# Rounded products for the RG-LRU gates and the mLSTM numerators, a last chunk through DRAM, and mixer blocks transposed a step later

## The chip, the cores and the metric

The kernel runs on one core of one Trainium2 chip. A time is the device time of one execution in microseconds. TensorE (PE) does the matrix products, VectorE (DVE), ScalarE (ACT) and GpSimd (POOL) the elementwise work, and SyncE (SP) starts the loads of the weights; GpSimd also starts some transfers of its own queue. All of them run at the same time and wait for one another by semaphores; each works through its own list in order.

## The reference

A decoder trunk of two layers works on 256 tokens of width 2048, batch 1, everything in fp32. Each layer takes an RMS norm, one combined input projection, token mixers, a gate, an output projection added to the residual, and then a gated embedding from a second input. Layer 0 has two mixers side by side on 1024 channels each: HGRN2 (a linear recurrence with a state matrix, in chunks of 64) and the RG-LRU:

```python
r  = sigmoid(einsum('bsnc,ncd->bsnd', xh, w_r) + b_r)     # 8 blocks of 128 x 128
ig = sigmoid(einsum('bsnc,ncd->bsnd', xh, w_i) + b_i)
log_a = -LRU_C * r * softplus(-lam)
a = exp(log_a);  u = sqrt(-expm1(2.0 * log_a)) * (ig * xf)
h_t = a_t * h_(t-1) + u_t
```

Layer 1 has an mLSTM of 8 heads (keys of 128, values of 256 channels): scores of queries and keys with a causal weight from two gates, a numerator (weights times values) and a denominator (the sum of the weights). The gate path is a product with SiLU of another projection.

## The kernel before, in words

Every weight matrix is read from HBM once, in halves of 128 x 1024 (`raw`, five buffers, L128). fp32 products are made of three products of a rounded format (fp32r): ScalarE rounds a half into `whi` (L131), VectorE subtracts to get the rest, `wlo` (L132); both have four buffers. The activations stand as pairs of the same kind (`ahl`, made by `split_act`: L145 rounds on ScalarE, L146 subtracts on VectorE). TensorE then adds up hi·hi, hi·lo and lo·hi. There are two forms. `block` makes 128 output channels by 256 tokens: sixteen matmuls of 512 columns (L161, weights hi against both halves of the activations), and sixteen of 256 (L167, weights lo). `quarter_tok` makes a quarter of the sum for 512 channels by 256 tokens: 24 matmuls of 512 columns (L225 to L227), twelve for each half of the tokens, from two weight halves. `project_tok` is four quarters, and `project_two` two chunks with the fourth quarters last.

The small work between is written as generators, one list of them per lane. `pump()` steps every lane once; it stands in the middle of each `block` and each `quarter_tok`. So the order of work around the products is set by how many `yield`s a generator has, and a tile scheduler then orders each engine's list by priority (weight splits have a raised one).

Layer 0 runs 32 blocks: the forget gates, queries and the RG-LRU inputs, between them two token-major chunks, then two chunks of the gate `ez` (`gate_tok`) and the other gate blocks (`gate_mul`), and the output projection `eo`. `rg_lru(r, xc)` runs for two halves of 512 channels. It loads the gates' weights `bw` (128 x 1024), waits a step (two for r = 1), and makes the gates in plain fp32: four matmuls at L823 for each of two `j`, an fp32 matmul being two records in the trace. After these come sigmoids (L827), exponentials (L833, L834) and the scan (L846).

`feature_major` turns a gated chunk of tokens by channels into channels by tokens: VectorE transposes blocks of 32 (L520), `across` writes it to DRAM and reads it back (L507, L510, on POOL's queue), and after a lag of five steps ScalarE applies a gain (L527) and it is split. Layer 1's last chunk goes another way, `feature_major_pe`: eight transposes on TensorE (L542), read from PSUM by the splits.

In layer 1 `mix(j)` (j = 0 to 3, two heads each) makes the causal weights `wt`, the scores (L1058, L1059), their product `scw`, and in the next step the numerators in plain fp32 (L1070, L1072: 257 columns, 256 values and a column of ones for the denominator). Values `vt` are written from the projection `ov` by ScalarE, the ones by POOL (L1099). After `oz`, the embedding's product (L338) runs, then `drain("fm0", ... "fm3")` finishes the chunks and `out_proj` multiplies with `oo`. POOL loads two rows of gains (`row`, L367) for L1151, which multiplies the embedding's values on VectorE while `oo` runs.

Of the kernel before, what the change touches and what calls it, by code (L numbers as in the profile page):

```python
# [19 lines left out]
P = 128  # L20
# [23 lines left out]
def trunk(ctx: ExitStack, tc: tile.TileContext, a, out):  # L44
# [368 lines left out]
    def out_proj(hq, w, y, lane):  # L413

        act = {}
        for c in range(4):
            ps = project_tok(w, c, y)
            with tc.high_priority(offset=100):
                for hf in range(2):
                    v.tensor_tensor(out=hq[c][:, hf], in0=ps[hf], in1=hq[c][:, hf], op=ALU.add)  # L420
            start(f"{lane}{c}", to_features(hq[c], c, act, None, lane))
            step(f"{lane}{c}")
        return act
# [91 lines left out]
    def feature_major(u, gain, first, y, room):  # L515

        w = room("w")
        w5 = w.rearrange("p (j c h t) -> p h c j t", j=4, c=4, h=2)
        for hf in range(2):
            v.transpose(w5[:, hf], u[:, hf].rearrange("p (c j q) -> p c j q", c=4, j=4))  # L520
        r = room("r")
        yield from across(w, r, f"du{gain}{first}", 5)
        r5 = r.rearrange("p (i c h t) -> p c h i t", i=4, c=4, h=2)
        for b in range(2):
            x = tp.tile([P, 512], F32, name="xr", tag="hn", bufs=3)
            for k in range(2):
                s.activation(x[:, k * T:(k + 1) * T].rearrange("p (h i t) -> p h i t", h=2, i=4), r5[:, 2 * b + k],  # L527
                             AF.Copy, scale=pc(gain, first + 2 * b + k))
            y[first // 2 + b] = split_act(x, "y")

    def feature_major_pe(u, gain, first, y):

        yield
        yield
        banks = []
        for b in range(2):
            ps = px.tile([P, 512], F32, name="mx", tag="mx")
            for k in range(2):
                c = (2 * b + k) * P
                for hf in range(2):  # L540
                    o = k * T + hf * P
                    te.transpose(ps[:, o:o + P], u[:, hf, c:c + P], ident)  # L542
            banks.append(ps)
        yield
        for b, ps in enumerate(banks):
            hi, lo, both = act_pair()
            for k in range(2):
                scaled_split(ps[:, k * T:(k + 1) * T], gain, first + 2 * b + k, hi[:, k], lo[:, k])
            y[first // 2 + b] = (hi, lo, both)
# [55 lines left out]
    with m0_scope:  # L605
# [203 lines left out]
        def rg_lru(r, xc):  # L809
# [6 lines left out]
            if r:  # L816
                yield
            for j in range(2):
                for w, (dst, bias) in enumerate(((av, "bbr"), (it, "bbi"))):
                    ps = px.tile([P, 512], F32, name="mx", tag="mx")  # L820
                    for i in range(2):
                        c = 2 * j + i
                        te.matmul(ps[:, i * T:(i + 1) * T], bw[:, w, c * P:(c + 1) * P], xc[:, c * T:(c + 1) * T],  # L823
                                  start=True, stop=True)
# [92 lines left out]
    act = out_proj(hq, a["eo"], y, "fe")  # L917
# [30 lines left out]
    with tc.tile_pool(name="m1", bufs=2) as m1:  # L948
# [39 lines left out]
        VW = 257  # L988
# [49 lines left out]
        def mix(j):  # L1038
# [15 lines left out]
            scw = room("scw")[:, 0:768].rearrange("p (i t) -> p i t", i=2)  # L1054
            for i in range(2):
# [7 lines left out]
            vt = vts[j]  # L1063
            nm = m1.tile([P, 2, 512], F32, name="num", tag="vt", bufs=6)
            for i in range(2):
                pool, tag = ((px, "mx"), (pst, "st"))[i]
                for hf in range(2):
                    c = hf * 8 + 2 * j + i
                    ps = pool.tile([P, 512], F32, name="nu", tag=tag)[:, 0:VW]
                    te.matmul(ps, scw[:, i, hf * P:(hf + 1) * P], vt[:, 0, i], start=True, stop=(hf == 0))  # L1070
                    if hf:
                        te.matmul(ps, scw[:, i, T:384], vt[:, 1, i], start=False, stop=True)  # L1072
                    o = nm[:, hf, i * 256:(i + 1) * 256]
                    s.copy(o, ps[:, 0:256])
                    v.tensor_copy(den[:, c:c + 1], ps[:, 256:VW])
# [20 lines left out]
        for j in range(4):  # L1096
            psv = project_tok(a["ov"], j, acth)
            vt = m1.tile([P, 2, 2, VW], F32, name="vt", tag="vt", bufs=6)
            gp.memset(vt[:, :, :, 256:VW], 1.0)  # L1099
            for hf in range(2):  # L1100
                s.activation(vt[:, hf, :, 0:256], psv[hf].rearrange("p (i e) -> p i e", i=2), AF.Copy,
                             scale=norm["rt"][:, hf:hf + 1])
            vts.append(vt)
# [18 lines left out]
        for j in range(4):  # L1122
# [8 lines left out]
            start(f"fm{j}", feature_major(u, "cn", 4 * j, y, room) if j < 3 else feature_major_pe(u, "cn", 4 * j, y))  # L1131
# [229 lines left out]
```

## Time and profile before

| what | us |
|---|---|
| median of 3 runs (lowest, highest) | 1051.79 (1050.85, 1053.89) |
| the profiled execution | 1051.14 |
| its span in the trace | 1049.4 |
| TensorE busy | 1038.6 |
| VectorE busy | 724.3 |
| ScalarE busy | 594.3 |
| GpSimd busy | 114.4 |

The span is one execution as the profiler saw it; some 1.7 us lie around it. The granted TensorE clock was 0.998 over the span. A row of the timeline has the start, the duration, the engine, the line of the code and the operation, what is written and read, and how many alike were joined; in brackets stands the idle time ahead of it and what ended it. A matmul's duration is modelled and longer than the distance to its successor, since matmuls overlap.

### The profile page before, as it was taken

What the parts mean: (1) busy time and instruction counts of PE and PEld (TensorE: products, weight loads), DVE (VectorE), ACT (ScalarE), POOL (GpSimd) and SP (SyncE); (2) the same over time, 40 slices, a digit from 0 to 9 for tenths busy, and PEclk for the clock granted to TensorE, in tenths of its full rate; (3) what the DMA queues carried; (4) which work ended last, traced back from release to release, by engine and by line L of the source; (5) the groups of instructions that cost most, each with busy time, mean ns of one, the idle gap of its engine ahead of it and who ended that gap; (6) DMA issues with size and microseconds to landing.
All of it is one profiled execution on the core that took longest, in us unless ns stands there. A gap on an engine that the chain in (4) does not pass through costs nothing.

```text
span 1049.4 us, 14961 instructions
## 1 busy us (share of the span) xinstructions
PE 1038.6 (99%) x5504; PEld 869.1 (83%) x5504; DVE 724.3 (69%) x1085; ACT 594.3 (57%) x893; POOL 114.4 (11%) x162
## 2 busy tenths in 40 slices
PE   9999999999999999999999999999999999999996
PEld 7888888888888888887888788888888888888886
DVE  6857897997877666766569864454457767666675
ACT  7775545869654444565557765544445565444553
POOL 0001232522201111111021000000001110111000
PEclk9999999999999999999999999999999999999999
DMA  9865544545867877687597644446557775977652
GB/s 350 311 205 192 172 164 157 182 150 192 275 234 258 249 247 230 212 277 235 177 271 248 203 169 160 161 161 201 199 188 225 250 262 187 294 239 242 201 181 81
DMA packets 64587, 225.40 MB, mean 215 GB/s; under 512 B 8065, under 2 KB 9345, under 8 KB 64513
## 3 DMA queue, kind: packets, MB, share of 16 engines
q1 hardware_dynamic: 55440, 196.38, 56.5%
q0 software_dynamic: 8496, 27.27, 8.6%
q8 instruction: 43, 0.70, 0.3%
q10 hardware_dynamic: 576, 0.79, 0.2%
q14 instruction: 32, 0.25, 0.1%
HBM read 211.30 MB, written 13.11 MB: 214 GB/s over the span
## 4 chain that ended last, share of the span: by engine, by line
PE 97%; DMA 1%; ACT 1%; DVE 0%; issue 0%; SPq 0%; ACTq 0%
PE mm L225 22%; PE mm L226 22%; PE mm L227 22%; PE mm L161 11%; PE mm L167 6%; PE mx L225 2%; PE mx L227 2%; PE mx L226 2%; PE mm L338 1%; DMA xq<-in_xT_dram 1%; PE mm L1196 1%; PE mm L1195 1%; PE mm L1194 1%; PE mx L823 1%; PE nu L1070 1%; PE mx L661 0%
## 5 line engine op out<-in xcount | busy, mean ns | idle before, releaser
L132 DVE TENSOR_TENSOR wlo<-raw,whi 128x1024 fp32r<-128x1024 f32 (+1 forms) x364 | 439.9, 1220 | 246.4 <-ACT whi L131 211.3
L131 ACT CAST whi<-raw 128x1024 fp32r<-128x1024 f32 (+1 forms) x364 | 378.3, 1043 | 356.4 <-PE mm L227 254.8
L225 PE MATMUL mm<-whi,ahl 128*128 128x512 f32 x1024 | 401.5, 392 | 0.0
L227 PE MATMUL mm<-whi,ahl 128*128 128x512 f32 x1024 | 398.5, 389 | 0.0
L226 PE MATMUL mm<-wlo,ahl 128*128 128x512 f32 x1024 | 398.4, 389 | 0.0
L225 PEld LDWEIGHTS mm<-whi,ahl 128*128 128x128 f32 x1024 | 192.2, 188 | 42.0 <-issue 2.1
L227 PEld LDWEIGHTS mm<-whi,ahl 128*128 128x128 f32 x1024 | 192.2, 188 | 40.5
L226 PEld LDWEIGHTS mm<-wlo,ahl 128*128 128x128 f32 x1024 | 192.3, 188 | 39.8 <-DVE wlo L132 0.5
L161 PE MATMUL mm<-ahl,whi 128*128 128x512 f32 x512 | 122.1, 390 | 0.0
L161 PEld LDWEIGHTS mm<-ahl,whi 128*128 128x128 f32 x512 | 94.2, 188 | 18.3
L167 PE MATMUL mm<-ahl,wlo 128*128 128x256 f32 x512 | 67.7, 285 | 0.0
L167 PEld LDWEIGHTS mm<-ahl,wlo 128*128 128x128 f32 x512 | 64.9, 191 | 2.2
L225 PE MATMUL mx<-whi,ahl 128*128 128x512 f32 x96 | 37.5, 391 | 0.0
L227 PE MATMUL mx<-whi,ahl 128*128 128x512 f32 x96 | 37.4, 389 | 0.0
L226 PE MATMUL mx<-wlo,ahl 128*128 128x512 f32 x96 | 37.3, 389 | 0.0
L507 POOL DMA_DIRECT2D ducn<-w x3 | 1.7, 561 | 206.2 <-DVE w L520 206.2
L173 ACT COPY sm<-mm 128x256 f32<-128x256 f32 x32 | 11.7, 366 | 19.1 <-PE mm L167 19.0
L225 PEld LDWEIGHTS mx<-whi,ahl 128*128 128x128 f32 x96 | 18.0, 188 | 3.7
L227 PEld LDWEIGHTS mx<-whi,ahl 128*128 128x128 f32 x96 | 18.0, 188 | 3.8
L226 PEld LDWEIGHTS mx<-wlo,ahl 128*128 128x128 f32 x96 | 18.0, 188 | 3.7
L971 DVE SCALAR_TENSOR_TENSOR qk<-xr,prm,qk 128x255 f32<-128x255 f32 (+2 forms) x48 | 20.4, 475 | 0.6 <-ACT qk L968 0.5
L1195 PE MATMUL mm<-wlo,ahl 128*128 128x256 f32 x64 | 18.1, 283 | 0.0
(304 smaller groups left out, 877.3 us busy)
## 6 DMA issues: line engine op xcount, KB each, us to landing
raw<-in_ew_dram SPq DMA_DIRECT2D x64, 512.0 KB, 4.4
raw<-in_g_dram SPq DMA_DIRECT2D x56, 512.0 KB, 4.7
raw<-in_eo_dram SPq DMA_DIRECT2D x32, 512.0 KB, 4.8
raw<-in_oqk_dram SPq DMA_DIRECT2D x32, 512.0 KB, 4.6
raw<-in_ov_dram SPq DMA_DIRECT2D x32, 512.0 KB, 3.8
raw<-in_oog_dram SPq DMA_DIRECT2D x32, 512.0 KB, 3.7
raw<-in_oz_dram SPq DMA_DIRECT2D x32, 512.0 KB, 4.2
raw<-in_oo_dram SPq DMA_DIRECT2D x32, 512.0 KB, 4.5
```

Of the source, the lines that this page charges most:

```text
L131: last["act"] = s.copy(h, r).ins
L132: last["dve"] = v.tensor_tensor(out=l, in0=r, in1=h.bitcast(F32), op=ALU.subtract).ins
L161: last["pe"] = te.matmul(ps, parts[k // 8][0][:, c:c + P], act[k // 2][2][:, (k % 2) * 512:(k % 2 + 1) * 512], start=(k == 0), stop=False).ins
L167: last["pe"] = te.matmul(ps[:, T:2 * T], parts[k // 8][1][:, c:c + P], act[k // 2][0][:, k % 2], start=False, stop=(k == KT - 1)).ins
L173: s.copy(small, ps[:, T:2 * T])
L225: te.matmul(ps[hf], xh, wh, start=(k == 0), stop=False)
L226: te.matmul(ps[hf], xh, wl, start=False, stop=False)
L227: last["pe"] = te.matmul(ps[hf], xl, wh, start=False, stop=(k == KT - 1)).ins
L338: last["pe"] = te.matmul(ps[hf], tokens(pact[x], k, hf), (hi, lo)[y][:, k * 512:(k + 1) * 512], start=(n == mine[0]), stop=(n == mine[-1]) ...
L823: te.matmul(ps[:, i * T:(i + 1) * T], bw[:, w, c * P:(c + 1) * P], xc[:, c * T:(c + 1) * T], start=True, stop=True)
L971: v.scalar_tensor_tensor(dst[:, sh:T], pi[:, 0:T - sh], pc("ccw", k * 16 + n), dst[:, sh:T], op0=ALU.mult, op1=ALU.add)
L1195: te.matmul(ps[hf], xh, wl, start=False, stop=False)
```

## The change

There are four parts. They touch the layer-0 gates, the layer-1 numerators, the last layer-1 chunk, and the two layer-0 chunks that go through DRAM.

1. In `rg_lru`, `bw` is split into a rounded part and a rest that take one `whi` and one `wlo` buffer, and the input `xc` is split into two pairs. The four plain matmuls for each `j` become twelve rounded ones (`mm3`), and they come one step later.
2. In `mix`, the weights `wt` are multiplied in place by the scores and split into `sh` and `sl`; the values are rounded as `vt`, with the rest in `vl`. Six matmuls for two heads become 18. The values have 258 columns now, two of them ones; the rest `vl` has 256.
3. `feature_major_pe` is gone: the last chunk goes through DRAM like the others. The output projection `oo` runs through `chunks`, which takes the first two chunks of output together, and steps a chunk's lane only where its values are needed.
4. The layer-0 chunks are transposed a step later, and the lag behind their transfer is four instead of five.

```diff
-    def out_proj(hq, w, y, lane):
+    def out_proj(hq, parts, lane):
         act = {}
-        for c in range(4):
-            ps = project_tok(w, c, y)
+        for c, ps in enumerate(parts):
...
-    def feature_major(u, gain, first, y, room):
+    def feature_major(u, gain, first, y, room, lag):
+        if lag < 5:
+            yield
         w = room("w")
...
-        yield from across(w, r, f"du{gain}{first}", 5)
+        yield from across(w, r, f"du{gain}{first}", lag)
...
-    def feature_major_pe(u, gain, first, y):
-        yield
-        yield
-        banks = []
-        for b in range(2):
-            ps = px.tile([P, 512], F32, name="mx", tag="mx")
-            for k in range(2):
-                c = (2 * b + k) * P
-                for hf in range(2):
-                    o = k * T + hf * P
-                    te.transpose(ps[:, o:o + P], u[:, hf, c:c + P], ident)
-            banks.append(ps)
-        yield
...
     def rg_lru(r, xc):
...
             if r:
                 yield
+            bh, bl = (wp.tile([P, 2, 512], F32R, name=n, tag=n) for n in ("whi", "wlo"))
+            s.copy(bh, bw)
+            v.tensor_tensor(out=bl, in0=bw, in1=bh.bitcast(F32), op=ALU.subtract)
+            xs = [split_act(xc[:, j * 512:(j + 1) * 512], "xc") for j in range(2)]
+            yield
...
-                        te.matmul(ps[:, i * T:(i + 1) * T], bw[:, w, c * P:(c + 1) * P], xc[:, c * T:(c + 1) * T],
-                                  start=True, stop=True)
+                        mm3(ps[:, i * T:(i + 1) * T], bh[:, w, c * P:(c + 1) * P], bl[:, w, c * P:(c + 1) * P], xs[j], i,
+                            True, True)
...
-                start(f"fm{g}", feature_major(u, "an", 4 * g, y, room0))
+                start(f"fm{g}", feature_major(u, "an", 4 * g, y, room0, 4))
...
-        VW = 257
+        VW = 258
...
-            scw = room("scw")[:, 0:768].rearrange("p (i t) -> p i t", i=2)
...
-                v.scalar_tensor_tensor(scw[:, i, :], sc[:, 0:384], SC, wt[:, i, :], op0=ALU.mult, op1=ALU.mult)
+                v.scalar_tensor_tensor(wt[:, i, :], sc[:, 0:384], SC, wt[:, i, :], op0=ALU.mult, op1=ALU.mult)
+            sh, sl = (bp.tile([P, 1024], F32R, name=n, tag="wt")[:, 0:768].rearrange("p (i t) -> p i t", i=2)
+                      for n in ("sh", "sl"))
+            s.copy(sh, wt)
+            v.tensor_tensor(out=sl, in0=wt, in1=sh.bitcast(F32), op=ALU.subtract)
             yield
...
-                    te.matmul(ps, scw[:, i, hf * P:(hf + 1) * P], vt[:, 0, i], start=True, stop=(hf == 0))
-                    if hf:
-                        te.matmul(ps, scw[:, i, T:384], vt[:, 1, i], start=False, stop=True)
+                    for b, o in ((0, hf * P), (1, T))[:1 + hf]:
+                        for x, y, n in ((sh, vh, VW), (sl, vh, VW), (sh, vl, T)):
+                            te.matmul(ps[:, 0:n], x[:, i, o:o + P], y[:, b, i], start=(b == 0 and x is sh and y is vh),
+                                      stop=(b == hf and y is vl))
...
-            vt = m1.tile([P, 2, 2, VW], F32, name="vt", tag="vt", bufs=6)
+            vt = m1.tile([P, 2, 2, VW], F32R, name="vt", tag="vt", bufs=6)
...
+                v.scalar_tensor_tensor(vl[:, hf], src, norm["rt"][:, hf:hf + 1], vt[:, hf, :, 0:256].bitcast(F32),
+                                       op0=ALU.mult, op1=ALU.subtract)
...
-            start(f"fm{j}", feature_major(u, "cn", 4 * j, y, room) if j < 3 else feature_major_pe(u, "cn", 4 * j, y))
+            start(f"fm{j}", feature_major(u, "cn", 4 * j, y, room, 5))
...
-        drain("fm0", "fm1", "fm2", "fm3")
+        step("fm3")
         start("emb", embed_norm())
-        act = out_proj(hq, a["oo"], y, "fo")
+        act = out_proj(hq, chunks(a["oo"], 4, y, ready(y, "fm")), "fo")
```

In TensorE's list, the gates of the first half (r = 0) move behind one more block. L661 and L642 are the same matmuls of the HGRN2 attention, L167 and L161 the blocks; L150 to L152 are the three lines of `mm3`:

```order
-L661 MATMUL mx<-q,k 32x48 x32
-L823 MATMUL mx<-xc,bw 128x256 x4
+L642 MATMUL mx<-q,k 32x48 x32
 L167 MATMUL mm<-ahl,wlo 128x256 x16
 L161 MATMUL mm<-ahl,whi 128x512 x16
-L823 MATMUL mx<-xc,bw 128x256 x4
+L150 MATMUL mx<-ahl,whi 128x256
+L151 MATMUL mx<-ahl,whi 128x256
+L152 MATMUL mx<-ahl,wlo 128x256
```

The first group stands where the second stood, and the second follows a block later.

In VectorE's list at that place the splits go in. Before, with L858 the convolution that makes the RG-LRU's input, L705, L699 and L700 HGRN2 work:

```order
L132 TENSOR_TENSOR wlo<-raw,whi 128x1024 x2
L858 SCALAR_TENSOR_TENSOR xc<-mg,prm,xc 128x253
L858 SCALAR_TENSOR_TENSOR xc<-mg,prm,xc 128x254
L174 TENSOR_TENSOR mg<-mm,sm 128x256
L858 SCALAR_TENSOR_TENSOR xc<-mg,prm,xc 128x253
L705 COPY_PREDICATED A_1852<-cst,mx 128x32x6
L699 TENSOR_TENSOR q<-f,tot_2155 128x32x16
L705 COPY_PREDICATED A_1852<-cst,mx 128x32x4
L700 TENSOR_TENSOR q<-q,tot_2155 128x32x8
L705 COPY_PREDICATED A_1852<-cst,mx 128x32x2
L132 TENSOR_TENSOR wlo<-raw,whi 128x1024 x2
```

After, where L844 is the convolution, L801 the rest of `bw`, L146 the rest of `xc`, L686 and L680 the HGRN2 work:

```order
L844 SCALAR_TENSOR_TENSOR xc<-mg,prm,xc 128x253 x2
L174 TENSOR_TENSOR mg<-mm,sm 128x256
L801 TENSOR_TENSOR wlo<-bw,whi 128x1024
L132 TENSOR_TENSOR wlo<-raw,whi 128x1024
L146 TENSOR_TENSOR ahl<-xc,ahl 128x2x256 x2
L686 COPY_PREDICATED A_1852<-cst,mx 128x32x6
L686 COPY_PREDICATED A_1852<-cst,mx 128x32x4
L686 COPY_PREDICATED A_1852<-cst,mx 128x32x2
L132 TENSOR_TENSOR wlo<-raw,whi 128x1024 x2
L174 TENSOR_TENSOR mg<-mm,sm 128x256
L680 TENSOR_TENSOR q<-f,tot_2155 128x32x16
```

Three splits stand ahead of HGRN2's work, and a weight split between them.

ScalarE's list in the second half (r = 1), before, from the first gates' sigmoids (L827) on; L787 and L790 copy and square HGRN2's output:

```order
L827 ACTIVATE av<-mx,prm 128x256 x2
L827 ACTIVATE it<-mx,prm 128x256 x2
L131 CAST whi<-raw 128x1024 x2
L556 ACTIVATE u<-mm,rth 128x512
L833 ACTIVATE tt<-av,sp_235 128x256 x2
L834 ACT_TABLE_LOAD
L834 ACTIVATE av<-av,spm_236 128x256
L787 COPY o<-mx 128x512
L790 ACTIVATE sq,hss<-mx 128x128 x4
L787 COPY o<-mx 128x512
L790 ACTIVATE sq,hss<-mx 128x128 x4
```

After; L800 rounds `bw`, L768 and L771 are what L787 and L790 were:

```order
L800 CAST whi<-bw 128x1024
L145 CAST ahl<-xc 128x2x256
L131 CAST whi<-raw 128x1024
L537 ACTIVATE u<-mm,rth 128x512
L768 COPY o<-mx 128x512
L771 ACTIVATE sq,hss<-mx 128x128 x4
L768 COPY o<-mx 128x512
L771 ACTIVATE sq,hss<-mx 128x128 x4
L131 CAST whi<-raw 128x1024 x2
L813 ACT_TABLE_LOAD
L813 ACTIVATE av<-mx,prm 128x256 x2
```

The sigmoids have moved behind HGRN2's output, and one of the two casts of weights that stood ahead of it too.

POOL's list around the last chunk, before; `ducn` are layer 1's chunks in DRAM, `dfo` those of the next stage:

```order
L507 DMA ducn_7550<-w 128x1024
L510 DMA r<-ducn_7550 32x4x256 x4
L367 DMA row<-in_rows_dram 128x1024 x2
L507 DMA dfo_8000<-w 128x1024
L510 DMA r<-dfo_8000 32x4x256 x4
L367 DMA row<-in_rows_dram 128x1024 x2
```

After:

```order
L506 DMA ducn_7674<-w 128x1024
L509 DMA r<-ducn_7674 32x4x256 x4
L506 DMA ducn_7922<-w 128x1024
L509 DMA r<-ducn_7922 32x4x256 x4
L367 DMA row<-in_rows_dram 128x1024 x4
L506 DMA dfo_8266<-w 128x1024
```

A fourth hop stands ahead of the row loads, and both pairs of rows follow it.

More of the change, by code (lines that the diff above doesn't have):

```diff
@@ L916, in trunk @@
     drain("pl")
-    act = out_proj(hq, a["eo"], y, "fe")
+    act = out_proj(hq, (project_tok(a["eo"], c, y) for c in range(4)), "fe")
     drain("pg")
@@ L1097, in trunk @@
             psv = project_tok(a["ov"], j, acth)
-            vt = m1.tile([P, 2, 2, VW], F32, name="vt", tag="vt", bufs=6)
-            gp.memset(vt[:, :, :, 256:VW], 1.0)
+            vt = m1.tile([P, 2, 2, VW], F32R, name="vt", tag="vt", bufs=6)
+            gp.memset(vt.bitcast(F32)[:, :, :, 256:VW], 1.0)
+            vl = ap.tile([P, 1024], F32R, name="vl", tag="ahl").rearrange("p (h i e) -> p h i e", h=2, i=2)
             for hf in range(2):
-                s.activation(vt[:, hf, :, 0:256], psv[hf].rearrange("p (i e) -> p i e", i=2), AF.Copy,
-                             scale=norm["rt"][:, hf:hf + 1])
-            vts.append(vt)
+                src = psv[hf].rearrange("p (i e) -> p i e", i=2)
+                s.activation(vt[:, hf, :, 0:256], src, AF.Copy, scale=norm["rt"][:, hf:hf + 1])
+                v.scalar_tensor_tensor(vl[:, hf], src, norm["rt"][:, hf:hf + 1], vt[:, hf, :, 0:256].bitcast(F32),
+                                       op0=ALU.mult, op1=ALU.subtract)
+            vts.append((vt, vl))
             for c in (j // 2, 2 + j // 2):
```

9 lines of the change are left out of this document (2 added, 7 removed).

## The prediction

> **What bounds the kernel now.** I read the page's busy times first, then its chain that ended last, then TensorE's rows in time around the places that the change touches.
>
> ```profile
> PE 1038.6 (99%) x5504; PEld 869.1 (83%) x5504; DVE 724.3 (69%) x1085; ACT 594.3 (57%) x893; POOL 114.4 (11%) x162
> PE 97%; DMA 1%; ACT 1%; DVE 0%; issue 0%; SPq 0%; ACTq 0%
> ```
>
> TensorE works 99% of the span, and 97% of the chain that ended last is its own matmuls. So a TensorE microsecond saved is a microsecond of the end, and anything that makes TensorE wait costs as much; the other engines have room on average, and the danger lies where they are locally full. Ends of matmuls are modelled, so I price by start-to-start distances.
>
> ```profile
> 185.80 2.08 PE L167 MATMUL mm<-ahl,wlo 128*128 128x256 f32 x16
> 187.71 3.81 PE L161 MATMUL mm<-ahl,whi 128*128 128x512 f32 x16
> 613.73 0.39 PE L227 MATMUL mm<-whi,ahl 128*128 128x512 f32 x1
> ...
> 615.77 0.39 PE L227 MATMUL mm<-whi,ahl 128*128 128x512 f32 x1
> 616.00 1.03 PE L1070 MATMUL nu<-vt,scw 128*128 128x257 f32 x4
> ...
> 618.41 0.58 PE L225 MATMUL mm<-whi,ahl 128*128 128x512 f32 x1
> 618.83 0.39 PE L226 MATMUL mm<-wlo,ahl 128*128 128x512 f32 x1
> ```
>
> Two prices: sixteen rounded 256-wide matmuls, each with its own weights, take 187.71 − 185.80 = 1.91 us, 0.1194 each. Nine rounded 512-wide ones take 615.77 − 613.73 = 2.04 us, 0.227 each.
>
> **The change, part by part.**
>
> *Numerators.* A head pair's six fp32 matmuls (twelve records) run from 616.00 to 618.41, 2.41 us, and the next 512-wide one takes 0.42 to its successor instead of 0.227: 0.19 more, together 2.60. There are four pairs (48 records in the groups below): 10.4 us. After: 4 × 18 rounded matmuls, 12 of them 258 wide: 72 × 0.12 = 8.6. Saving 1.8 us.
>
> ```profile
> L1070 PE MATMUL nu<-vt,scw 128*128 128x257 f32 x32 | 8.2, 379 | 0.0
> L823 PE MATMUL mx<-xc,bw 128*128 128x256 f32 x32 | 7.7, 382 | 0.0
> L1072 PE MATMUL nu<-vt,scw 128*128 128x257 f32 x16 | 4.8, 379 | 0.0
> L542 PE MATMUL mx<-cst,u 128*128 128x128 f32 x8 | 1.2, 273 | 0.0
> ```
>
> *Gates.* 32 records are 16 fp32 matmuls in four groups of eight records, one of them here:
>
> ```profile
> 241.29 1.89 PE L823 MATMUL mx<-xc,bw 128*128 128x256 f32 x8
> 242.83 0.58 PE L225 MATMUL mm<-whi,ahl 128*128 128x512 f32 x1
> 243.25 0.39 PE L226 MATMUL mm<-wlo,ahl 128*128 128x512 f32 x1
> ...
> 858.59 0.60 PE L542 MATMUL mx<-cst,u 128*128 128x128 f32 x4
> 858.94 0.48 PE L338 MATMUL mm<-whi,ahl 128*128 128x512 f32 x1
> 859.26 0.40 PE L338 MATMUL mm<-wlo,ahl 128*128 128x512 f32 x1
> ```
>
> A group costs 242.83 − 241.29 = 1.54, and 0.19 behind it: 1.73, four 6.9. After: 48 × 0.1194 = 5.7. Saving 1.2 us.
>
> *Transposes.* Four of the eight take 858.94 − 858.59 = 0.35 and 0.09 behind; both groups 0.9 us, all saved on TensorE. Sum for TensorE: 1.8 + 1.2 + 0.9 = 3.9; I take 3.8, since the 258-wide ones are a shade dearer than the 256-wide price.
>
> The Trainium skill, "FP8 and Floating Point Precision", section TensorE Precision Notes, counts a true fp32 product as four passes, so three rounded products would be three quarters of it: numerators and gates 17.3 to 13.0 us, a saving of 4.3 instead of 3.0. The rows here disagree with so clean a ratio (0.1194 against a quarter of 0.43, which is 0.108); the sum keeps the rows.
>
> *What is added elsewhere.* VectorE and ScalarE get the splits: two of bw, four pairs of xc, sh and sl, vl. By these rows a half-width split is 0.61 on ScalarE and 0.69 on VectorE:
>
> ```profile
> L146 DVE TENSOR_TENSOR ahl<-xr,ahl 128x512 fp32r<-128x512 f32 x18 | 12.2, 685 | 2.6 <-ACT ahl L145 2.6
> L145 ACT CAST ahl<-xr 128x512 fp32r<-128x512 f32 x18 | 10.9, 612 | 0.1
> 190.00:198.00 8.00, 8.00 (x104) 6.88 (x103) 8.00 (x15) 7.94 (x15) 3.11 (x2) 1.00 0.48 169
> ```
>
> Some 15 us of VectorE in all: free unless a weight split is late by it. In the mix the pairs are 1.9 us ahead of their use and nothing else is full there, so I take nothing; a wait there is bounded by one cast and one subtract of 768 columns, about 2 us.
>
> *First RG-LRU half (r = 0).* Here VectorE is busy all 8.00 us of 190 to 198 and ScalarE 7.94 (third and fourth pairs of the row). The gates' splits (1.23 + 2 × 0.69 = 2.6 us of VectorE) go in there, and the first gates come one step later, about 198. Late by 0 to 2.6; the order puts the splits ahead of L680/L681 (before: L699/L700, 1.1 us) and of three L686, so I take 0.
>
> *Second half (r = 1).* bw's halves hold one of four whi and one of four wlo buffers until the last gates, so weight halves turn over in three. The rows of this stretch:
>
> ```profile
> 238.61 1.05 PE L783 MATMUL mx<-vt,A 128*128 128x128 f32 x8
> 241.06 0.39 PE L786 MATMUL mx<-vt,A 128*128 128x128 f32 x2
> 240.28 0.57 ACT L787 COPY o<-mx 128x512 f32<-128x512 f32 x1
> 243.14 0.27 ACT L790 ACTIVATION_READ_ACCUMULATOR sq<-mx 128x1 f32 x1
> 245.09 1.04 ACT L131 CAST whi<-raw 128x1024 fp32r<-128x1024 f32 x1
> 243.44 0.17 DVE L791 TENSOR_SCALAR hss<-hss 128x8 f32<-128x8 f32 x1 [2.93 <-ACT sq L790]
> 244.46 0.17 DVE L238 SCALAR_TENSOR_TENSOR hnr<-hnt,hnr 128x8 f32<-128x8 f32 x1
> 246.16 1.23 DVE L132 TENSOR_TENSOR wlo<-raw,whi 128x1024 fp32r<-128x1024 f32 x1
> ```
>
> In the new order the gates no longer follow L783/L786 (now L764/L767); twelve matmuls of a quarter's second half follow. The next quarter's second weight half gets its buffer after six of these (1.36 us after the group's end, 241.29), but its cast stands on ScalarE behind the L787/L790 chain, which ends at 243.41, 2.12 after. Cast 1.04, and on VectorE the seven small instructions of L791 to L238 end at 244.63, 3.34 after, then 1.23: ready at 4.6. TensorE reads that wlo 12 + 6 + 1 = 19 matmuls after the group, 19 × 0.227 = 4.3. Late by 0.3. The next two such halves wait for TensorE and have 13 × 0.227 − 1.04 − 1.23 = 0.7 to spare if both engines are free. I take 0.3 us, between 0 and 2.
>
> *Fourth gate chunk through DRAM.* On POOL's queue the hop now stands ahead of the rows that L1144 (before: L1151) multiplies, and VectorE works in order: two weight splits wait behind L1144.
>
> ```profile
> 837.03 0.56 POOL L507 DMA_DIRECT2D ducn<-w  x1 [15.87 <-DVE w L520]
> 840.92 2.18 POOL L510 DMA_DIRECT2D r<-ducn  x4 [3.33 <-DMA ducn<-w]
> 843.09 1.11 POOL L367 DMA_DIRECT2D row<-in_rows_dram  x2
> DMA to landing us min/median/max: 6.2/8.8/11.2
> 860.22 1.21 DVE L132 TENSOR_TENSOR wlo<-raw,whi 128x1024 fp32r<-128x1024 f32 x1
> 867.39 0.68 DVE L1151 TENSOR_TENSOR pl<-pl,row 128x512 f32<-128x512 f32 x1
> 875.82 2.59 DVE L132 TENSOR_TENSOR wlo<-raw,whi 128x1024 fp32r<-128x1024 f32 x2 [1.61 <-ACT whi L131]
> 881.34 0.39 PE L225 MATMUL mm<-whi,ahl 128*128 128x512 f32 x1
> 322.15 0.69 DVE L374 TENSOR_TENSOR pl<-pl,row 128x512 f32<-128x512 f32 x1 [3.49 <-DMA row<-in_rows_dram]
> ```
>
> The new chunk's transposes end by about 861.4 (the end of the split at 860.22). As at 837, out 3.9 and back 2.2 us: the rows are issued at about 867.5 and land 6.2 to 11.2 later, 873.7 to 878.7. Then two L1144 (1.3) and a split (1.2): the half that TensorE first reads behind 881.34 (0.2 later, its wlo) is ready at 876.2 to 881.2. So this wait, which stood at layer 0 too (3.49 at 322.15), is hidden: 0, at most 0.5. The chunk's own values are needed at the seventh quarter of the projection, some 30 us on. The second pair of row loads moves ahead of L506's next hop, which is itself later.
>
> *First mixer blocks a step later.* They are read at the same step as before; the hop has one step (about 5.5 us) less and four left. 0.
>
> **Sum.** −3.8 + 0.3 = −3.5 us. The profiled execution took 1051.14 (span 1049.4): 1047.6. The runs' median, 1051.79, lies 0.65 above it: **1048.3**.
>
> **Rivals.**
>
> A. *Starved halves.* The three late halves at r = 1 each meet a 1.2 us VectorE row or a 1.28 table load and are 0.6 late, the first more: 1.5 to 2.5 in all, 1049.8 to 1050.8. For it: three buffers where four were; against: 0.7 to spare in two of three.
>
> B. *Gates wait for their own splits* at r = 0, up to 2.6: 1048.6 to 1050.9. For it: the full VectorE; against: rows moved behind.
>
> C. *Rows behind the hop*, the other side: TensorE waits at the second quarter of the last projection. It eats the gain if the rows land 15 us after issue, and gives 1055 at 18. For it: four hop reads and the weight stream share the DMA engines; against: 11.2 is the longest landing.
>
> D. *Weight loads exposed.* 80 weight loads (records above) become 120. At 0.19 each, 40 more cost 7.6: 1055.9. Against it: L167's sixteen matmuls, each with its load, in 1.91 us. The Trainium skill, "TensorE: Matmul & The Clock Gate", part on row/col tiling, says that loads overlap matmuls in flight only when the row group differs; by that rule this rival would hold, and the trace's 83% of PEld beside 99% of PE speaks against it.
>
> E. *Three passes for four*, exactly, as if each record's fixed cost vanished: 1.3 us more gain, 1047.0. Against it: 0.1194 at L167.
>
> **Chances.** Forecast 0.47 (nearly all of it faster by over 0.3%, which is 3.15 us and about what a measurement of this kernel can tell from no change: below 1048.6), A 0.26, B 0.10, C 0.06, D 0.05, E 0.06. Faster 0.49 (forecast 0.43, E); same 0.41 (A, B, the forecast's rest, a little of C); slower 0.10 (D, C). Range: from E's edge, 1046.8, up over A and B to 1053.0, which leaves out D, most of C and little else.
>
> **What would show it.** Right: L150 to L152 as mx and L1061 at 0.12 us start to start; no L542; TensorE's idle time under 1 us between 180 and 330, and L1144 waiting for rows for 4 to 10 us without a TensorE gap at 878. Wrong: TensorE waiting for wlo at ez's second chunk by more than 1 us, a gap ahead of the gates near 198, a gap behind L1144, or 0.13 and more per rounded matmul.

## The result

The changed kernel took 1046.15 us in the median of six runs (1046.08 to 1046.24), the kernel before 1051.36 in six runs taken with it (1050.85 to 1053.89). The ratio is 0.9945 with a 95% interval from 0.9932 to 0.9957: faster by 0.55%, where 0.33% was forecast (1048.3) and 1046.8 was the lower end of the range. The direction was right, the size was not, and the time lies 0.65 us below the range.

A larger number of runs of the kernel before, taken beside the experiments, gives medians of 1050.37 (33 runs), 1050.43 (19) and 1050.55 (21). Against these the gain is 4.2 to 4.4 us; a second set of the changed kernel had 1046.22 (five runs, ratio 0.9954, interval 0.9942 to 0.9966). So the first six runs of before were about 1 us high, and part of the miss is there.

The page of the changed kernel, busy times and chain:

```profile
PE 1034.2 (99%) x5536; PEld 867.6 (83%) x5536; DVE 736.5 (71%) x1103; ACT 597.6 (57%) x903; POOL 113.4 (11%) x167
PE 99%; DMA 0%; ACT 0%; SPq 0%; issue 0%; DVE 0%; ACTq 0%
```

TensorE is still the whole chain, and has lost 4.4 us of busy time. VectorE has 12 us more of its own, which cost TensorE no more than the 0.21 us shown below.

Both kernels run the same large products in the same order up to the last projection, so the same product stands in both traces, and the difference of the two starts tells what was gained up to there. Worked out from the starts in the two profiled executions:

| up to | before | after | gained so far | in this stage |
|---|---|---|---|---|
| third product of the first block of quarters (L227) | 18.20 | 17.64 | 0.56 | 0.56 |
| last weight product ahead of the RG-LRU gates (L161) | 191.14 | 190.59 | 0.55 | 0 |
| behind the gates (L225) | 253.93 | 252.44 | 1.49 | 0.94 |
| ahead of the first numerators (L227) | 615.77 | 614.33 | 1.44 | −0.05 |
| behind the last numerators (L226) | 699.50 | 696.19 | 3.31 | 1.87 |
| ahead of the embedding's product (L227) | 852.74 | 849.42 | 3.32 | 0 |
| in the projection `oo` (L226) | 866.59 | 862.11 | 4.48 | 1.16 |
| one of the last products (L1196, now L1189) | 1040.25 | 1035.76 | 4.49 | 0 |
| end of the span | 1049.35 | 1044.46 | 4.89 | 0.40 |

Of 4.89 us, 3.97 lie at the three places of the change, 0.56 in the first 18 us and 0.40 behind the last product, at two places that the change doesn't touch.

### The profile page after: what moved, and what is told of

It is laid out like the page before. It is cut to its first block, busy times and chain, and to the rows that moved or that the text cites. A ratio compares the mean times of both kernels' runs of the same rounds, so it can differ in the third digit from the quotient of the medians.

```text
span 1044.5 us, 15072 instructions
## 1 busy us (share of the span) xinstructions
PE 1034.2 (99%) x5536; PEld 867.6 (83%) x5536; DVE 736.5 (71%) x1103; ACT 597.6 (57%) x903; POOL 113.4 (11%) x167
## 4 chain that ended last, share of the span: by engine, by line
PE 99%; DMA 0%; ACT 0%; SPq 0%; issue 0%; DVE 0%; ACTq 0%
PE mm L225 22%; PE mm L226 22%; PE mm L227 22%; PE mm L161 11%; PE mm L167 6%; PE mx L226 3%; PE mx L225 3%; PE mx L227 3%; PE mm L338 2%; PE nu L1061 1%; PE mm L1189 1%; PE mm L1188 1%; PE mm L1187 1%; PE mx L642 0%; DMA raw<-in_pw_dram 0%; PE mx L764 0%
## 5 line engine op out<-in xcount | busy, mean ns | idle before, releaser
L225 PE MATMUL mm<-whi,ahl 128*128 128x512 f32 x992 | 388.0, 391 | 0.0
L226 PE MATMUL mm<-wlo,ahl 128*128 128x512 f32 x992 | 386.1, 389 | 0.0
L227 PE MATMUL mm<-whi,ahl 128*128 128x512 f32 x992 | 386.0, 389 | 0.0
L225 PEld LDWEIGHTS mm<-whi,ahl 128*128 128x128 f32 x992 | 186.2, 188 | 40.8 <-issue 2.1
L227 PEld LDWEIGHTS mm<-whi,ahl 128*128 128x128 f32 x992 | 186.2, 188 | 38.9
L226 PEld LDWEIGHTS mm<-wlo,ahl 128*128 128x128 f32 x992 | 186.3, 188 | 38.4 <-DVE wlo L132 0.5
L161 PE MATMUL mm<-ahl,whi 128*128 128x512 f32 x512 | 122.1, 390 | 0.0
L161 PEld LDWEIGHTS mm<-ahl,whi 128*128 128x128 f32 x512 | 94.2, 188 | 18.3
L167 PE MATMUL mm<-ahl,wlo 128*128 128x256 f32 x512 | 67.3, 284 | 0.0
L167 PEld LDWEIGHTS mm<-ahl,wlo 128*128 128x128 f32 x512 | 64.8, 191 | 2.0
L225 PE MATMUL mx<-whi,ahl 128*128 128x512 f32 x128 | 50.0, 391 | 0.0
L227 PE MATMUL mx<-whi,ahl 128*128 128x512 f32 x128 | 49.8, 389 | 0.0
L226 PE MATMUL mx<-wlo,ahl 128*128 128x512 f32 x128 | 49.8, 389 | 0.0
L227 PEld LDWEIGHTS mx<-whi,ahl 128*128 128x128 f32 x128 | 24.0, 188 | 5.0
L225 PEld LDWEIGHTS mx<-whi,ahl 128*128 128x128 f32 x128 | 24.0, 188 | 5.0
L226 PEld LDWEIGHTS mx<-wlo,ahl 128*128 128x128 f32 x128 | 24.0, 188 | 4.9
```

Source lines behind the costliest of these rows:

```text
L161: last["pe"] = te.matmul(ps, parts[k // 8][0][:, c:c + P], act[k // 2][2][:, (k % 2) * 512:(k % 2 + 1) * 512], start=(k == 0), stop=False).ins
L167: last["pe"] = te.matmul(ps[:, T:2 * T], parts[k // 8][1][:, c:c + P], act[k // 2][0][:, k % 2], start=False, stop=(k == KT - 1)).ins
L225: te.matmul(ps[hf], xh, wh, start=(k == 0), stop=False)
L226: te.matmul(ps[hf], xh, wl, start=False, stop=False)
L227: last["pe"] = te.matmul(ps[hf], xl, wh, start=False, stop=(k == KT - 1)).ins
```

## The places, as the profile after shows them

The numerators of one pair of heads on TensorE, in time (start, duration):

```profile
614.33 0.39 PE L227 MATMUL mm<-whi,ahl 128*128 128x512 f32 x1
614.56 0.28 PE L1061 MATMUL nu<-vt,sh 128*128 128x258 f32 x1
614.68 0.28 PE L1061 MATMUL nu<-vt,sl 128*128 128x258 f32 x1
...
616.58 0.28 PE L1061 MATMUL nu<-vl,sh 128*128 128x256 f32 x1
616.70 0.40 PE L225 MATMUL mm<-whi,ahl 128*128 128x512 f32 x1
616.93 0.39 PE L226 MATMUL mm<-wlo,ahl 128*128 128x512 f32 x1
```

Eighteen products from 614.56 to 616.70: 2.14 us, 0.119 each, and the next wide one takes its usual 0.23. The 0.19 us behind an fp32 group is gone with it. Before, 2.60.

The second RG-LRU half, where three buffers were left for the weights. TensorE, then VectorE, then ScalarE:

```profile
242.53 0.39 PE L225 MATMUL mm<-whi,ahl 128*128 128x512 f32 x1
242.85 0.50 PE L226 MATMUL mm<-wlo,ahl 128*128 128x512 f32 x1
243.18 0.40 PE L227 MATMUL mm<-whi,ahl 128*128 128x512 f32 x1
243.42 0.39 PE L225 MATMUL mm<-whi,ahl 128*128 128x512 f32 x1
240.48 0.16 DVE L772 TENSOR_SCALAR hss<-hss 128x8 f32<-128x8 f32 x1
241.49 0.17 DVE L238 SCALAR_TENSOR_TENSOR hnr<-hnt,hnr 128x8 f32<-128x8 f32 x1
241.57 1.22 DVE L132 TENSOR_TENSOR wlo<-raw,whi 128x1024 fp32r<-128x1024 f32 x1
240.10 1.08 ACT L131 CAST whi<-raw 128x1024 fp32r<-128x1024 f32 x1
```

The wait that the prediction worked out is there, and at the weight half it named: the cast starts at 240.10 as HGRN2's output leaves ScalarE, the small instructions of VectorE follow from 240.48 to 241.6, the split ends at 242.79, and L226 starts at 242.85 instead of 242.76. From L225 to the next L225 pass 0.89 us instead of 0.68: 0.21 lost, where 0.3 was put.

The rows behind the fourth chunk's hop, on POOL and VectorE:

```profile
857.18 0.56 POOL L506 DMA_DIRECT2D ducn<-w  x1 [17.40 <-DVE w L521]
861.97 2.18 POOL L509 DMA_DIRECT2D r<-ducn  x4 [4.23 <-ACT whi L131]
864.14 2.15 POOL L367 DMA_DIRECT2D row<-in_rows_dram  x4
871.15 1.29 DVE L1144 TENSOR_TENSOR pl<-pl,row 128x512 f32<-128x512 f32 x2 [2.34 <-DMA row<-in_rows_dram]
872.36 1.22 DVE L132 TENSOR_TENSOR wlo<-raw,whi 128x1024 fp32r<-128x1024 f32 x1
```

The rows land 7.0 us after their issue, VectorE waits 2.34 us for them, and the split behind is done at 873.6, some 3.5 us ahead of its use in this kernel's time. The list of TensorE's waits has nothing there:

```profile
PE st L95 <- POOL ones L90: 1.1, 1, 1.1
PE mx L338 <- ACT whi L131: 0.7, 2, 0.5
```

Both are in the first 8 us (engine, line, what ended the wait; us in total, times, the longest).

## The experiments

The theory at the outset: each part gains what its rows say, and the rest lies in the start and end of the execution. The rivals: a part gains more than its rows say; or the gain is what the other parts hide.

### The rounded gates alone

```diff
 the kernel before, with of the change only:
+            bh, bl = (wp.tile([P, 2, 512], F32R, name=n, tag=n) for n in ("whi", "wlo"))
+            s.copy(bh, bw)
+            v.tensor_tensor(out=bl, in0=bw, in1=bh.bitcast(F32), op=ALU.subtract)
+            xs = [split_act(xc[:, j * 512:(j + 1) * 512], "xc") for j in range(2)]
+            yield
...
+                        mm3(ps[:, i * T:(i + 1) * T], bh[:, w, c * P:(c + 1) * P], bl[:, w, c * P:(c + 1) * P], xs[j], i,
+                            True, True)
```

> The kernel before with the rounded gates alone (part 1). Theory of the parts (each part saves on TensorE what its own rows say, and the rest of the measured gain lies in the start and the end of the execution, which no part touches): -0.9 us, that is 1.2 saved in four groups less 0.2 to 0.3 waited at the second weight half of ez's second chunk; against the fastest runs of before (1050.9) about 1050.0. Rival (the whole gain is the parts' doing): more than 1.2 us. Rival A (starved weight halves): with the transposes a step earlier than in the changed kernel VectorE is fuller at ez, and the wait there grows to 1 us or more, so that nothing is gained.

1050.52 us in the median of 11 runs, ratio 0.9999 (0.9990 to 1.0008): no gain that can be told from none. The trace shows why. By 229 us the first half has gained 0.6 us; by 254 this and 0.2 more are gone again. (The end of this execution is 0.40 us shorter than that of before, and 0.53 more are lost at 856 us; both come up again below.) TensorE's list of waits:

```profile
PE mm L226 <- DVE wlo L132: 1.1, 1, 1.1
```

So starved halves (rival A) decide here, though not in the whole change. What differs is part 4.

### The changed kernel without the later transposes

```diff
-                start(f"fm{g}", feature_major(u, "an", 4 * g, y, room0, 4))
+                start(f"fm{g}", feature_major(u, "an", 4 * g, y, room0, 5))
```

> The changed kernel with the layer-0 mixer blocks transposed at the old step (part 4 undone). Theory of the cover (with bw's halves in the weight buffers, the transposes at the old step stand ahead of a weight split on VectorE, and part 4 moves them out of the way): TensorE waits for wlo in ez's second chunk for 1.1 to 1.4 us as with the rounded gates alone, so 1.0 to 1.2 us slower than the changed kernel. Rival (part 4 is worth nothing, as the prediction had it, and the wait of the rounded gates alone came of another cause): within 0.2 us of the changed kernel.

1047.24 us (five runs, 1046.90 to 1047.29) beside 1046.22 for the changed kernel on the same chip: 1.0 us slower in the median. Product for product 1.17 us are lost, all of it at one place. VectorE and TensorE of this kernel:

```profile
239.40 0.69 DVE L872 TENSOR_TENSOR u<-u,o 128x512 f32<-128x512 f32 x1
240.00 1.30 DVE L521 STREAM_TRANSPOSE wu<-u 128x512 f32<-128x512 f32 x2
242.20 0.17 DVE L238 SCALAR_TENSOR_TENSOR hnr<-hnt,hnr 128x8 f32<-128x8 f32 x1
242.28 1.22 DVE L132 TENSOR_TENSOR wlo<-raw,whi 128x1024 fp32r<-128x1024 f32 x1
243.56 0.50 PE L226 MATMUL mm<-wlo,ahl 128*128 128x512 f32 x1 [1.11 <-DVE wlo L132]
```

The two transposes (1.30 us) stand ahead of the small instructions and the split. In the changed kernel they come behind the split that starts at 241.57:

```profile
242.79 0.70 DVE L521 STREAM_TRANSPOSE wu<-u 128x512 f32<-128x512 f32 x1
244.59 0.70 DVE L521 STREAM_TRANSPOSE wu<-u 128x512 f32<-128x512 f32 x1
```

Part 4 on its own is worth nothing (next run) and with the gates a full microsecond.

### The later transposes alone

```diff
+        if lag < 5:
+            yield
...
-        yield from across(w, r, f"du{gain}{first}", 5)
+        yield from across(w, r, f"du{gain}{first}", lag)
...
+                start(f"fm{g}", feature_major(u, "an", 4 * g, y, room0, 4))
```

> The kernel before with the layer-0 mixer blocks transposed a step later (part 4). Theory of the parts: 0 within 0.2 us. Rival: it takes scatter away, so that the slow half of the runs of before (1051.8 to 1053.9) is not seen: the median falls by 0.5 us or more though the fastest run does not.

1050.27 us (11 runs), ratio 1.0002 (0.9993 to 1.0011). No effect, and the scatter stayed: its profiled run was its longest, 1052.93, and shows where that run lost its time. First the list of TensorE's waits, then ScalarE's timeline:

```profile
PE mm L338 <- ACT pl L349: 1.1, 1, 1.1
PE mm L338 <- DVE u L559: 1.0, 1, 1.0
```

```profile
851.18 1.31 ACT L529 ACTIVATE xr<-r,prm 128x256 f32<-128x256 f32 x3 [3.13 <-DMA r<-ducn]
853.32 0.67 ACT L558 ACTIVATE u<-mm,rth 128x512 f32<-128x512 f32 x1
```

ScalarE stands for 3.13 us at the read-back of the third chunk (`r<-ducn`), and the gate's eviction (L558) and the embedding's (L349) are queued behind it. TensorE waits for both evictions and loses 2.5 us more than before between 852 and 865. In the profile of before the same wait is shorter, and it is there in the numerators alone and the gates alone too (lines of before, p2_num and p1_gates):

```profile
849.39 1.31 ACT L527 ACTIVATE xr<-r,prm 128x256 f32<-128x256 f32 x3 [0.61 <-DMA r<-ducn]
846.33 1.31 ACT L527 ACTIVATE xr<-r,prm 128x256 f32<-128x256 f32 x3 [0.37 <-DMA r<-ducn]
850.06 1.31 ACT L527 ACTIVATE xr<-r,prm 128x256 f32<-128x256 f32 x3 [1.15 <-DMA r<-ducn]
```

Counted by TensorE's products, ScalarE comes to this read-back at the same point in all four, so the wait is as long as the transfer is late. The same products without the wait take 12.69 us in the changed kernel, and 0.91 more with the transposes. Against these 13.61, TensorE lost 0.10 us where ScalarE waited 0.37, 0.25 where it waited 0.61, 0.78 for 1.15 and 2.75 for 3.13.

### The rounded numerators alone

```diff
 the kernel before, with of the change only the lines in mix, vt and vl:
+            sh, sl = (bp.tile([P, 1024], F32R, name=n, tag="wt")[:, 0:768].rearrange("p (i t) -> p i t", i=2)
+                      for n in ("sh", "sl"))
...
+                        for x, y, n in ((sh, vh, VW), (sl, vh, VW), (sh, vl, T)):
```

> The kernel before with the rounded numerators alone (part 2). Theory of the parts: -1.9 us (four groups of 18 matmuls at 0.12 instead of 2.6 us each). The rival that three passes cost exactly three quarters of four: -2.6. The rival that weight loads are exposed: +3 or more.

1049.15 us (11 runs, 1047.75 to 1050.91), ratio 0.9987 (0.9978 to 0.9996): 1.2 us in the median, 2.1 between the shortest runs. In its trace, that of its shortest run, the numerators gain 1.87 and the end 0.41. The spread of 3 us is the read-back's, by the theory; the run of the numerators with the pairs tests this.

### The last chunk and the pairs alone

```diff
-            start(f"fm{j}", feature_major(u, "cn", 4 * j, y, room) if j < 3 else feature_major_pe(u, "cn", 4 * j, y))
+            start(f"fm{j}", feature_major(u, "cn", 4 * j, y, room, 5))
...
-        drain("fm0", "fm1", "fm2", "fm3")
+        step("fm3")
...
-        act = out_proj(hq, a["oo"], y, "fo")
+        act = out_proj(hq, chunks(a["oo"], 4, y, ready(y, "fm")), "fo")
```

> The kernel before with the last chunk through DRAM and the projection oo in pairs of chunks (part 3). Theory of the parts: -1.2 us on TensorE between the gate chunk and the projection, no wait behind the multiplication with the rows. Rival: the end of the execution gains too (0.4 us in the profile after), so -1.6. Rival C (rows behind the hop): TensorE waits at the second quarter of oo, 0 or slower.

1049.24 us (11 runs, 1048.72 to 1049.86), ratio 0.9987 (0.9978 to 0.9995): 1.1 us. In the trace 1.16 us are gained between 852 and 865, and TensorE waits for nothing there. The end is 0.41 shorter too, as the rival had it; an interval of 0.5 to 2.3 us can't tell 1.2 from 1.6.

### The pairs with the transposes still on TensorE

```diff
-        drain("fm0", "fm1", "fm2", "fm3")
+        step("fm3")
...
-        act = out_proj(hq, a["oo"], y, "fo")
+        act = out_proj(hq, chunks(a["oo"], 4, y, ready(y, "fm")), "fo")
```

> The kernel before with the projection oo in pairs of chunks that step a chunk's lane only when it is needed, but the last chunk still transposed on TensorE (half of part 3). Theory of the late hop (the scatter of the kernel before sits at 850 us, where ScalarE stands in its list at the read-back of the third chunk, which has only just landed, with the gate's and the embedding's evictions behind it; the pairs move that read-back behind the embedding): the highest runs, 1051 to 1053, are gone, TensorE waits for no eviction between 848 and 865, the median falls by 0.3 to 0.6 us, and the transposes still cost their 0.9. Rival (the scatter comes with the transposes themselves): the spread stays and the median is that of before.

1050.36 us (11 runs, 1049.97 to 1050.62), ratio 0.9996 (0.9988 to 1.0005). No run lies far above the others, but of the 19 runs of before beside them only one does (1054.13), so eleven can't show that such runs are gone. As the late hop says, the read-back is now behind the embedding's evictions in ScalarE's list, and TensorE's only waits lie in the start; ScalarE in the changed kernel, where it is the same:

```profile
859.36 0.59 ACT L349 COPY pl<-mm 128x512 f32<-128x512 f32 x1 [0.31 <-PE mm L338]
861.68 1.31 ACT L528 ACTIVATE xr<-r,prm 128x256 f32<-128x256 f32 x3
```

But the median didn't fall by 0.3 to 0.6; it fell by 0.07. So in most runs of before the read-back cost little. The eight transposes, now together, cost 0.91 us against the changed kernel, product for product.

### The numerators with the pairs

```diff
 the numerators' lines as above, and:
-        drain("fm0", "fm1", "fm2", "fm3")
+        step("fm3")
...
-        act = out_proj(hq, a["oo"], y, "fo")
+        act = out_proj(hq, chunks(a["oo"], 4, y, ready(y, "fm")), "fo")
```

> The kernel before with the rounded numerators and with the projection oo in pairs of chunks (the last chunk still transposed on TensorE). Theory of the late hop (the rounded numerators alone gave 1.2 us in the median and 2.2 in the fastest run because the read-back at 850 us came late more often): the spread shrinks to 0.7 us as with the pairs alone, and the median is 1.85 below that of the pairs alone, 1048.5. Rival (the numerators really gain only 1.2 us): 1049.1, spread as with the numerators alone.

1048.07 us (11 runs, 1047.57 to 1048.61), ratio 0.9977 (0.9968 to 0.9986). The spread fell from 3.2 to 1.0 us, and the median lies 2.3 below that of the pairs alone. 1.87 of that is the numerators, product for product; 0.47 is at the end of the execution, of which more below. So the missing part of the numerators' gain comes back when the read-back moves. That it was lost there is likely and not shown, since no long run of the numerators alone has a trace. Of all 54 runs of the kernels with the pairs, except the one with a buffer of its own for both halves (its highest lies 1.5 us above), none lies more than 0.7 us above its kernel's median; of the 73 runs of before beside the experiments, seven do.

### More transfers ahead of the read-back

```diff
         gp.dma_start(out=d, in_=w)
+        if name == "ducn8":
+            for n in range(2):
+                gp.dma_start(out=dr.tile([P, 1024], F32, name=f"more{n}"), in_=w)
```

> The kernel before with two more writes of the third chunk to DRAM (512 KB each, never read) on POOL's queue ahead of its read-back, so that the read-back lands later. Theory of the late hop: ScalarE waits at 850 us by so much longer, TensorE waits for the evictions behind it, and every run is 2 to 5 us slower, with the loss between 852 and 865 us. Rival (the read-back has slack and the scatter has another cause): within 0.5 us of before.

1051.65 us (10 runs) against 1050.55, ratio 1.0009 (1.0000 to 1.0018): slower by 1.1 us in the median, which is the direction of the late hop but less than expected. In its profiled run ScalarE waits 1.87 us for the read-back instead of 0.61, TensorE 0.59 us for an eviction. The two writes delayed the landing by little more than a microsecond. ScalarE's list is not quite that of before here: the gate's eviction stands behind two of the four instructions of the read-back, in before behind all four. So this isn't the old wait made longer and nothing else.

### The fourth chunk through DRAM without the pairs

```diff
 the changed kernel, with
-        step("fm3")
+        drain("fm0", "fm1", "fm2", "fm3")
...
-        act = out_proj(hq, chunks(a["oo"], 4, y, ready(y, "fm")), "fo")
+        act = out_proj(hq, a["oo"], y, "fo")
```

> The changed kernel with oo's chunks one by one and all lanes emptied ahead of them, as before, but the last chunk through DRAM (the other half of part 3 undone). Theory of the late hop: the third chunk's read-back stands at 850 us again, so the scatter is back, and ScalarE meets the fourth chunk's read-back (landing about 870) ahead of weight casts: 0.5 to 3 us slower than the changed kernel, with TensorE waiting behind 870. Rival (the pairs only change the order of output): within 0.3 us of it.

1046.05 us (four runs, 1045.86 to 1046.12): the same as the changed kernel, so the expectation was wrong, at least for these few runs. Counted by TensorE's products, ScalarE comes to the third read-back at the same point as in before, where it began to wait at 848.78. In this execution the transfer had landed by then, and it waited for nothing; at the fourth it waited:

```profile
845.14 1.31 ACT L529 ACTIVATE xr<-r,prm 128x256 f32<-128x256 f32 x3
871.89 0.51 ACT L529 ACTIVATE xr<-r,prm 128x256 f32<-128x256 f32 x1 [3.75 <-DMA r<-ducn]
```

A wait of 3.75 us on ScalarE there costs TensorE 0.14 us. That the pairs are needed for the gain is not shown; four runs can't tell whether a rare long one is still there.

### A buffer of its own for the rounded half of bw

```diff
-            bh, bl = (wp.tile([P, 2, 512], F32R, name=n, tag=n) for n in ("whi", "wlo"))
+            bh = m0.tile([P, 2, 512], F32R, name="bwh", tag="bwh", bufs=1)
+            bl = wp.tile([P, 2, 512], F32R, name="wlo", tag="wlo")
```

> The changed kernel with a buffer of its own for the rounded half of bw, so that whi keeps its four (wlo still lends one). Theory of the three buffers (the 0.2 us that TensorE waits at 243 in the changed kernel is the cast that stands behind HGRN2's output on ScalarE because its buffer came free late): no wait there, 0.2 us faster. Rival (the wait is VectorE's own): no change.

1048.21 us (eight runs), 2.0 slower. At 243 the wait is gone (0.2 us gained there), but with other buffers the scheduler wrote another list for the first half too. ScalarE's timeline there, and TensorE's list of waits:

```profile
201.03 1.05 ACT L131 CAST whi<-raw 128x1024 fp32r<-128x1024 f32 x1 [3.80 <-DMA raw<-in_ez_dram]
```

```profile
PE mm L226 <- DVE wlo L132: 1.6, 1, 1.6
```

ScalarE, working in order, stood 3.8 us at a cast whose raw data had not landed, and all that followed came late; TensorE lost 1.9 us at 210. Where the free buffer was, was right; what the list did with it was not.

### The same for the second half alone

```diff
-            bh, bl = (wp.tile([P, 2, 512], F32R, name=n, tag=n) for n in ("whi", "wlo"))
+            bh = m0.tile([P, 2, 512], F32R, name="bwh", tag="bwh", bufs=1) if r else wp.tile([P, 2, 512], F32R, name="whi", tag="whi")
+            bl = wp.tile([P, 2, 512], F32R, name="wlo", tag="wlo")
```

> The changed kernel with a buffer of its own for the rounded half of bw in the second half (r = 1) alone; in the first it takes a whi buffer as in the changed kernel, so the list there stays as it was. Theory of the three buffers: the 0.2 us at 243 are gone and no wait comes at 210: 1046.0, 0.2 us faster than the changed kernel. Rival (the scheduler's list moves elsewhere too and gives it back): the same or slower.

1045.99 us (five runs, 1045.87 to 1046.55) beside 1046.22 for the changed kernel in another group: the 0.21 us at 243 are gained, product for product, and the list at 210 stayed. In the profiled run, the longest of the five, 0.13 were given back at 250 and 0.25 to 0.38 from 323 on, where VectorE waits for the rows of layer 0, so that its trace shows no gain in all. It is the lowest median of all kernels tried, but u_pairs is as low within 0.1, and 0.2 us is hardly more than two groups of the changed kernel differ by.

### The changed kernel once more

> The changed kernel itself once more, as the measure for the others of this group. Theory of the starts (the first 18 us differ by up to 0.9 us from one execution to the next, whatever the kernel): its runs spread over 0.5 to 1 us from about 1045.5 to 1046.5, and the first product of a quarter starts within 16.8 to 17.5 us. Rival (the changed kernel has a shorter start of its own): all of them within 0.2 us and the same start as in the first profile.

1046.22 us (1045.77 to 1046.47, five runs); no line is changed. Its first quarter started at 17.07 us, against 17.16 and 17.43 in the profiles of after and before. At the three places of the change it gains 0.95, 1.88 and 1.16 us, within 0.01 of the first profile.

### What the fourteen profiles say of start and end

The third product of the first quarter began anywhere from 17.19 us (u_lag) to 18.20 (before), with no order by kernel. TensorE's waits there are for the first weights (0.6 us for `wlo` in before, 0.7 for `whi` in after).

The end does go by kernel. From the end of the last matmul to the end of the span, four kernels took 8.82 to 8.88 us (before, p4_lag, p3_pairs, hop_more), the other ten 8.40 to 8.43. The difference lies in the output's own transfer: its last packet on queue q1 ended 7.31 to 7.33 us behind the last matmul in the four, 6.76 to 6.77 in the others. The DMA queues in the last 10 us of before, and of after (packets, MB, share):

```profile
q1 hardware_dynamic: 1296, 1.84, 44.8%
q10 hardware_dynamic: 144, 0.26, 6.3%
q14 instruction: 1, 0.01, 0.3%
```

```profile
q1 hardware_dynamic: 1296, 1.84, 46.9%
q10 hardware_dynamic: 144, 0.26, 6.5%
```

Those four, and none of the others, have one transfer of instructions on the queue q14 in their last 8 us. Fourteen of fourteen fit, so the 0.4 us go with that fetch; that the fetch is what delays the output's last packets is likely, but only argued. The Trainium skill, "Runtime: NRT & Kernel Launch", section Instruction fetch mechanics, says that an engine's instructions are fetched in blocks of 256 and that crossing a boundary is mostly hidden. In these traces the end is 0.4 us longer where a fetch falls into it. That a change elsewhere in the kernel moved a boundary there, and that this fetch was not hidden, no run here shows by itself.

## Why the prediction was right or wrong

*The sum for TensorE (−3.8): right.* The numerators gained 1.87 (1.8 put). The gates gained 0.94 with their wait of 0.21, so 1.15 without it (1.2 put). The transposes cost 0.91 (0.9 put). Both prices, 0.12 for a rounded 256-wide matmul with its weights and 0.19 behind an fp32 group, came from start-to-start distances in the trace of before and held. Rivals D (exposed weight loads) and E (three quarters exactly) are refuted by the 0.119 of L1061.

*The wait at r = 1 (0.3): right in place and nearly in size, 0.21*, since it was worked out in the new order of the lists.

*"First mixer blocks a step later ... 0": wrong as a price of that part.* On its own it is 0; in the company of the gates it is worth 1.0 us, because it takes 1.3 us of transposes from in front of the split that is late already. The sum was not hurt, since the 0.3 already had part 4 in it, but a reader who had left part 4 out by that line would have lost the gates' whole gain. Rival A was the right mechanism and needed part 4 undone to decide.

*First half, r = 0 (0) and rows behind the hop (0): right.* TensorE begins the gates at 197.39 as the block before ends; VectorE's 2.34 us of waiting for the rows are hidden, with 3.5 us to spare.

*"The runs' median, 1051.79, lies 0.65 above it: 1048.3": wrong.* This is the step that failed: the level of before from which the saving was taken. It used the median of three scattered runs as the level of the kernel, and carried their excess over to the changed one. The 73 further runs of before have medians of 1050.37 to 1050.55; from there −3.5 would have given 1046.9 to 1047.1, in the range and 0.7 to 0.9 above the measured time. The scatter has a place that the trace of before showed (ScalarE's 0.61 us of waiting for `r<-ducn` at 849, ahead of two evictions), and the prediction priced the third part without looking at what it does to that wait. But why three of the first six runs of before were above 1051 us, and only seven of the 73, stays open: none of those runs has a trace.

*Not in the sum at all:* 0.40 us at the end of the execution, which the sum put at nothing without a reason and which goes with an instruction fetch; and 0.25 us of the profiled execution of before at that read-back (1.16 gained at the place, 0.91 of it transposes). The 0.56 us at the start belong to no kernel: in fourteen profiles that product begins anywhere within 1.0 us.

The account against larger groups: 1.87 + 0.94 + 0.91 + 0.40 = 4.1 of 4.2 to 4.4 us. Of the 2.15 us between forecast and measurement, 1.2 to 1.4 are the level, 0.2 the three places (3.7 for 3.5) and 0.4 the end; 0.1 to 0.3 stay open.

## What to carry to other kernels

Where one engine is the chain, price each edit by start-to-start distances on it, and take the sum from the level of many runs, not from the median of a few. Scatter can have a place in the trace (here an engine that works in order and stands at a transfer's landing, with evictions behind it), so ask of each part what it does to that wait. A step that "costs nothing" should be priced beside the part that fills its neighbourhood: undo it in the full change, not only add it alone.

## What was not expected of the hardware

Three rounded matmuls of 256 columns (0.36 us) are 0.83 of one in fp32 (0.433 with its share of what follows), and the 0.09 to 0.19 us that follow an fp32 group are part of that price. A single instruction fetch in the last 8 us goes with 0.4 us of the end. ScalarE's waiting for a DRAM read-back cost TensorE 0.1 to 0.25 us where it lasted 0.37 to 0.61, and 2.75 us in the one long execution that has a trace, where it lasted 3.13.
